# Twelve input-projection tiles per layer computed by the seven-product scheme, in a phase of their own ahead of the mixers (two-layer hybrid trunk, one core)

## The chip, the cores and the metric

The kernel runs on one core of one Trainium2 chip. The metric is device time in microseconds (us). The kernel before takes 1718.01 us (median of 3 runs, 1717.88 to 1718.38). One execution was taken by the hardware profiler; its rows are what the text quotes. PE is the matrix engine (PEld its weight loads), DVE the vector engine, ACT the scalar engine, POOL GpSimd, SP the engine that issues most DMAs. A name such as ACTq is the instruction queue of that engine.

## The reference

Two identical layers work on `x` of 512 tokens by 1024 features in float32:

```python
h = rms_norm(x, ln1[l])
x = x + mixer_block(h, ...)       # u = h @ w_in, four causal mixers, gates, w_up_*, w_out
h = rms_norm(x, ln2[l])
x = x + swiglu(h, w_ffn_in[l], w_ffn_out[l])
...
u = h @ w_in
(fq, fk, fv, ff, gq, gk, gv, glr, gr, rq, rk, rv, rg, z, xbc, dt, gates) = split_cols(u, IN_SPLITS)
...
merged = (g[:, :, 0] * (y_a @ w_up_a) + g[:, :, 1] * (y_b @ w_up_b)
          + g[:, :, 2] * (y_c @ w_up_c) + g[:, :, 3] * (y_d @ w_up_d))
return merged @ w_out
```

The columns of `w_in` feed a forgetting attention (FoX, branch A: fq, fk, fv), a gated linear attention (GLA, B: gq, gk, gv, gr), a retention (C: rq, rk, rv, rg), a Mamba-2 scan (SSD, D: z, and xbc, which passes a four-tap causal convolution per channel), and four sigmoid gates of 1024 columns each. The hidden width of the SwiGLU is 2816.

## The kernel before, in words

Activations lie feature-major: a tile holds 128 features by 512 tokens. PE multiplies a 128x128 block of weights (the stationary side) with such a tile, and a column tile of `w_in` (128 of its columns) takes eight blocks. For precision each product is made three times (`mm3`, L200): every operand is split (`split`, L211) into a high part, a cast to the rounded format fp32r on ACT, and a low part, a subtraction on DVE; PE does high x high, high x low and low x high. One plain column tile is thus 24 matmuls of 512 columns.

Weights stream from HBM in slabs of 8 blocks (512 KB), in the order in which the program asks for them. `load` (L245) puts the DMA on SP's queue into one of two `wr` buffers, `convert` (L257) makes the two parts (ACT, then DVE: lines L212 and L213), `block` (L273) hands a block to PE, and `ahead` keeps two slabs converted in advance.

The input of a layer is normalised late: PE multiplies `x` times the gain (`xh`, `xl`, made by `Norm.feed`, L392, one feature tile at a time), and the row factor 1/rms (`n1.r`: squares, a tree of additions, a matmul with ones, some Newton steps, L366 to L372) is multiplied into each result afterwards. So the first group of four column tiles (`group`, L426) can start while `x` still arrives.

A layer runs as follows.

1. The first group: the four x tiles of xbc (`ps4`, L497). In layer 0 its hook also issues squares and constants. Then `n1.rstd`.
2. Two more xbc tiles, each convolution (`conv`, L475: one tensor-scalar and three multiply-adds on DVE, a Silu on ACT), and the four z tiles, in turns: `proj`, `conv`, `proj`, `conv`. In layer 0 `rotary` (L352) computes the tables of sines. Then the token-major columns (`wide`, L286).
3. The mixers `ssd`, `gla`, `ret`, `fox` are generators with many small steps. `drain` (L462) steps through one, and after each step `pull` (L455) takes fillers from the list `fill` until they are worth `PACE` microseconds: projections (`keep`, `tokmajor`, `silus`), gates (`gate_quad`, L1145: four column tiles and a Sigmoid over all four) and up-projections (`ups`, L1160: a product with `w_up_*`, times the gate, added into `merged`). The fillers give PE work while a mixer's chain is on DVE and ACT.
4. After `fox` the remaining fillers are worked off (L1196): the last four gate tiles of branch A and its eight up-projections, which need FoX's result `ya`. Then `w_out` and the residual.
5. The SwiGLU. Its first four column tiles are plain. The other twenty pairs go in units of four column tiles through the Strassen-Winograd scheme (`strassen`, L1253): a 2x2 arrangement of quarters of the weights and of `x` is multiplied with seven products in place of eight. Each product is 24 `mm3`-matmuls on 256 columns, 168 in a unit. Before that, `sums` (L1226) makes the four combinations t1 to t4 of the input's quarters: eight scales on ACT, eight subtractions of 128x512 on DVE, and four splits. It runs in the hook at k=4 of the plain group. For each unit four quads of 512 KB are loaded (`load(u)`: three `rq` buffers and one `wr` buffer); products 1, 2 and 4 use a quad as it is, with its low part made by ACT (L1286) and an accumulating DMA issued on POOL (L1287); products 6, 5, 7 and 3 use sums made on DVE (L1277) and then split. `collect` copies and adds the results out of PSUM (L1349 on ACT; additions on DVE).

Within each engine a scheduler sets the final order from the program's order and its own estimate of the times; the engines wait for each other by semaphores.

## Time and profile before

| | |
|---|---|
| median of 3 runs | 1718.01 us (1717.88 to 1718.38) |
| time of the profiled execution | 1718.72 us |
| span of the profiled execution | 1717.0 us |
| granted TensorE clock, mean | 0.999 |
| PE busy | 1705.9 us, 99% of the span |
| DVE busy | 1213.2 us, 71% |
| ACT busy | 861.9 us, 50% |
| POOL busy | 225.2 us, 13% |
| moved by DMA | 195.00 MB, mean 114 GB/s |

The span runs from the first to the last event in the trace; 1.7 us of the execution's time lie around it. Busy times overlap between engines. In the rows of a timeline, the columns are start and duration in us, the engine, the line of the kernel, the operation, what it writes and reads by the program's names, and in brackets how long the engine was idle before it and which event ended that. Rows of the chain of waits are start, duration, engine, line and number of instructions. Where consecutive matmuls overlap in the pipeline, their durations exceed their spacing, so a matmul's price is read from the spacing or from a row of the chain that spans many of them. In layer 0 `w_out` lies from 485 to 527 us and the SwiGLU behind it; layer 1 begins at 860.4 us.

### The profile page before, as it was taken

What the parts mean: (1) busy time and instruction counts of PE and PEld (TensorE: products, weight loads), DVE (VectorE), ACT (ScalarE), POOL (GpSimd) and SP (SyncE); (2) the same over time, 40 slices, a digit from 0 to 9 for tenths busy, and PEclk for the clock granted to TensorE, in tenths of its full rate; (3) what the DMA queues carried; (4) which work ended last, traced back from release to release, by engine and by line L of the source; (5) the groups of instructions that cost most, each with busy time, mean ns of one, the idle gap of its engine ahead of it and who ended that gap; (6) DMA issues with size and microseconds to landing.
All of it is one profiled execution on the core that took longest, in us unless ns stands there. A gap on an engine that the chain in (4) does not pass through costs nothing.

```text
span 1717.0 us, 25146 instructions
## 1 busy us (share of the span) xinstructions
PE 1705.9 (99%) x10140; PEld 1484.7 (86%) x10140; DVE 1213.2 (71%) x1683; ACT 861.9 (50%) x1190; POOL 225.2 (13%) x227
## 2 busy tenths in 40 slices
PE   8999999999999999999999999999999999999998
PEld 7878888888888999998988788888888889999998
DVE  5867666768677677675777666767776677767666
ACT  5424543546447646464544254435553574655543
POOL 2032110022101010101010322200221010101010
PEclk9999999999999999999999999999999999999999
DMA  5322222222235657575333222222222365665653
GB/s 199 106 74 74 75 82 78 86 86 74 78 112 143 196 134 186 135 186 121 89 99 115 68 74 75 85 76 89 83 86 82 103 172 161 152 175 139 183 108 102
DMA packets 54693, 195.00 MB, mean 114 GB/s; under 512 B 6064, under 2 KB 6448, under 8 KB 54576
## 3 DMA queue, kind: packets, MB, share of 16 engines
q1 hardware_dynamic: 45072, 160.45, 29.2%
q0 software_dynamic: 8640, 31.46, 10.3%
q8 instruction: 79, 1.29, 0.3%
q10 hardware_dynamic: 864, 1.48, 0.2%
q14 instruction: 38, 0.31, 0.1%
HBM read 191.27 MB, written 2.10 MB: 113 GB/s over the span
## 4 chain that ended last, share of the span: by engine, by line
PE 97%; DVE 1%; DMA 1%; ACT 1%; issue 0%; ACTq 0%; DVEq 0%
PE mm L198 65%; PE mx L198 31%; PE mx L1079 0%; DMA x<-in_x_dram 0%; DMA t<-in_ext_dram 0%; ACT wh L212 0%; DVE wl L213 0%; PE mx L679 0%; DVE t L369 0%; ACT L231 0%; DVE t L836 0%; ACT g L236 0%; DVE t L1168 0%; DVE n L407 0%; PE mx L871 0%
## 5 line engine op out<-in xcount | busy, mean ns | idle before, releaser
L212 ACT CAST wh<-wr 128x1024 fp32r<-128x1024 f32 (+1 forms) x240 | 250.0, 1043 | 378.4 <-PE mm L198 238.0
L198 PE MATMUL mm<-xh,wh 128*128 128x512 f32 (+1 forms) x1184 | 429.2, 362 | 0.9 <-DVE t L1168 0.9
L198 PE MATMUL mm<-xh,wl 128*128 128x512 f32 (+1 forms) x1184 | 428.6, 362 | 0.0
L198 PE MATMUL mm<-xl,wh 128*128 128x512 f32 (+1 forms) x1184 | 427.4, 361 | 0.0
L213 DVE TENSOR_TENSOR wl<-wr,wh 128x1024 fp32r<-128x1024 f32 (+1 forms) x220 | 281.8, 1282 | 119.9 <-ACT wh L212 117.6
L198 PEld LDWEIGHTS mm<-xh,wh 128*128 128x128 f32 x1184 | 222.6, 188 | 35.2 <-DVE t L1168 1.8
L198 PEld LDWEIGHTS mm<-xh,wl 128*128 128x128 f32 x1184 | 222.6, 188 | 35.1 <-issue 1.5
L198 PEld LDWEIGHTS mm<-xl,wh 128*128 128x128 f32 x1184 | 222.6, 188 | 33.7 <-issue 1.1
L198 PE MATMUL mm<-t,wh 128*128 128x512 f32 x448 | 140.3, 392 | 0.0
L198 PE MATMUL mx<-xh,wh 128*128 128x256 f32 (+1 forms) x448 | 136.2, 311 | 3.0 <-ACT wh L212 3.0
L198 PE MATMUL mx<-xl,wh 128*128 128x256 f32 (+1 forms) x448 | 138.5, 309 | 0.0
L1287 POOL DMA_DIRECT2D wl<-in_wsq_dram x60 | 51.9, 864 | 518.0 <-ACT wl L1286 337.1
L198 PE MATMUL mx<-f,wh 128*128 128x512 f32 x352 | 108.3, 390 | 0.0
L198 PE MATMUL mm<-f,wh 128*128 128x512 f32 x352 | 106.0, 390 | 0.0
L198 PEld LDWEIGHTS mm<-t,wh 128*128 128x128 f32 x448 | 83.3, 188 | 17.1
L213 DVE TENSOR_TENSOR l<-rq,wh 128x1024 fp32r<-128x1024 f32 x60 | 73.2, 1219 | 33.1 <-ACT wh L212 18.7
L198 PEld LDWEIGHTS mx<-xh,wh 128*128 128x128 f32 x448 | 84.1, 188 | 9.2 <-ACT wh L212 4.0
L198 PE MATMUL mx<-xh,wl 128*128 128x256 f32 (+1 forms) x288 | 91.0, 327 | 0.0
L198 PEld LDWEIGHTS mx<-xl,wh 128*128 128x128 f32 x448 | 84.2, 188 | 5.1
L198 PE MATMUL mm<-t,wl 128*128 128x512 f32 x224 | 87.5, 390 | 0.0
L212 ACT CAST wh<-rq 128x1024 fp32r<-128x1024 f32 x60 | 62.9, 1049 | 43.9 <-PE mm L198 21.5
L198 PEld LDWEIGHTS mm<-f,wh 128*128 128x128 f32 x352 | 66.1, 188 | 13.5
(275 smaller groups left out, 3457.2 us busy)
## 6 DMA issues: line engine op xcount, KB each, us to landing
wr<-in_wst_dram SPq DMA_DIRECT2D x216, 512.0 KB, 3.5
rq<-in_wsq_dram SPq DMA_DIRECT2D x60, 512.0 KB, 5.3
wl<-in_wsq_dram POOLq DMA_DIRECT2D x60, 512.0 KB, 7.1
wr<-in_wsq_dram SPq DMA_DIRECT2D x20, 512.0 KB, 7.3
out_dram<-x SPq DMA_DIRECT2D x8, 256.0 KB, 2.0
x<-in_x_dram SPq DMA_DIRECT2D x3, 512.0 KB, 7.2
wr<-in_wst_dram SPq DMA_DIRECT2D x4, 256.0 KB, 5.6
x<-in_x_dram SPq DMA_DIRECT2D x2, 256.0 KB, 4.5
```

The costliest lines, as they stand in the source:

```text
L198: T.matmul(o, lhsT=l, rhs=r, start=start, stop=stop, skip_group_check=True)
L212: A.copy(out=hi, in_=src)
L213: V.tensor_tensor(out=lo, in0=src, in1=hi.bitcast(F32), op=ALU.subtract)
L1287: G.dma_start(out=lo, in_=wsq[j], accum_op=ALU.add)
```

## The change

Twelve of a layer's plain `w_in` column tiles go through the seven-product scheme, as three units of four: (x4, x5 | z0, z1), (z2, z3 | gq0, gq1), (gk0, gk1 | gr0, gr1). They run in a phase ahead of the mixers, right behind the first group of four x tiles.

- `strassen`, `sums` and `rights` (the table of right-hand sides, earlier inside `layer`) become functions for either matrix. In the front phase t4 has buffers of its own, since `x` times gain (`xh`, `xl`) is needed afterwards; in the SwiGLU it overwrites a quarter of it, as before.
- The hook of the first group, at k=4, does the squares and constants (layer 0 only) and then `sums(tb1, ...)` and `begin(-2)`: the loads of the first unit's quads and the early low parts.
- The three units follow, then the six convolutions one behind the other, then the token-major columns, and the mixers. In layer 0 `rotary` stands right ahead of `drain(ssd(), ...)`.
- The front phase needs buffers: `front()` opens an outer set (`kp`, eight tiles of 128x2x512) and an inner one (`tq`, `ep`, `rp`, `lp`) that is closed before the mixers. The eight tiles of `kp` hold first the scaled inputs and sums, then the units' results, then, two columns at a time, gates and the merged sum (before: `gp`, tiles of four). The pool of the mixers' tiles falls from 33 to 24.
- Since gq, gk and gr are there already, the fillers shift forward: gates of branch D and rv, rg ahead of `ssd`; one gate quad of branch A (`gate_quad(0, 1)`) goes from behind `fox` to ahead of `drain(fox(), ...)`; `PACE` falls by 7 to 8%.
- 24 quads join the stream of quads (80 to 104), and 12 slabs a layer leave the plain stream.

The core of the diff:

```diff
-PACE = (4.5, 5.0, 5.0, 7.5)
+PACE = (4.2, 4.6, 4.6, 6.9)
...
-FRONT = 26 * 8 + 24 + 2 * 16 + 32 * 8 + 80 + 64 + 2 * PLAIN * KD
+FRONT = 14 * 8 + 24 + 2 * 16 + 32 * 8 + 80 + 64 + 2 * PLAIN * KD
...
-QUADS = DEPTH * (NF - PLAIN) // 2 * 4
+QUADS = DEPTH * (3 + (NF - PLAIN) // 2) * 4
...
-    def mixers():
-        return phase(gp=2, vp=2, bd=1, tp=33)
+    def front():
+        outer = phase(g=64, kp=8)
+        return outer, phase(tq=1, ep=4, rp=5, gl=64, lp=2)
...
+        def front_done(u, a, b):
+            both(a)
+            both(b, 0.125 if u == 1 else None)
+            if u == 0:
+                cin[4:6] = a[:, 0], a[:, 1]
+                act(out=b, in_=b, func=AF.Silu)
+                sz[:2] = b[:, 0], b[:, 1]
...
+        cols = [(C_X + 4 * P, C_Z), (C_Z + 2 * P, C_GQ), (C_GK, C_GR)]
+        begin, run = strassen("w_in", l, [tuple(pairs_of(c) for c in u) for u in cols], tb1, KT, True, front_done)
...
         def first():
-            for k in range(KD):
-                n1.square(k)
-            constants()
-
-        ps4 = group("w_in", l, [C_X + P * i for i in range(4)], n1, KD, first if l == 0 else None)
+            if l == 0:
+                for k in range(KD):
+                    n1.square(k)
+                constants()
+            sums(tb1, PR("ln1"), KT)
+            begin(-2)
+
+        ps4 = group("w_in", l, [C_X + P * i for i in range(4)], n1, KD, first)
         n1.rstd(True)
...
+        run()
+        scope.close()
+        scope = phase(vp=2, bd=1, tp=24)
...
         for i in (4, 5, 0, 1, 2, 3):
-            cin[i] = scaled(ps4[i] if i < 4 else proj("w_in", l, C_X + P * i, n1, KD))
-        conv(4, cin[4])
-        conv(5, cin[5])
-        for i in range(4):
-            sz[i] = scaled(proj("w_in", l, C_Z + P * i, n1, KD))
-            act(out=sz[i], in_=sz[i], func=AF.Silu)
             conv(i, cin[i])
...
-        fill += [keep(gq, j, C_GQ + P * j, 0.125) for j in range(2)] + [keep(gk, j, C_GK + P * j) for j in range(2)]
-        fill += silus([C_GR, C_GR + P, C_RG, C_RG + P])
+        fill += gate_quad(3, 0) + tokmajor(rv, C_RV) + silus([C_RG, C_RG + P])
         fill += [keep(rq, j, C_RQ + P * j) for j in range(2)] + [keep(rk, j, C_RK + P * j) for j in range(2)]
+        if l == 0:
+            rotary()
         drain(ssd(), PACE[0])
...
-        fill += mix(gate_quad(2, 0), up_of(1, 1)) + mix(gate_quad(2, 1), up_of(2, 0)) + mix(gate_quad(0, 0), up_of(2, 1))
+        fill += mix(gate_quad(2, 0), up_of(1, 1)) + mix(gate_quad(2, 1), up_of(2, 0)) + mix(gate_quad(0, 0), up_of(2, 1)) + gate_quad(0, 1)
         drain(fox(), PACE[3])
-        fill += mix(gate_quad(0, 1), up_of(0, 0)) + up_of(0, 1)
+        fill += up_of(0, 0) + up_of(0, 1)
```

How the order on the engines changes is shown at three places. The first is PE at the start of layer 0, behind the first group. Before, the sum for 1/rms (`mm_315`, `mm_322`) is followed by the next plain projection (`mm_342`), whose right-hand sides `xh`, `xl` the first group has used already:

```order
L198 MATMUL mm_315<-n_316,cr 128x512
L198 MATMUL mm_315<-n_317,cr 128x512
L198 MATMUL mm_322<-cs,n_222 128x1 x4
L198 MATMUL mm_342<-xh_134,wh_287 128x512
L198 MATMUL mm_342<-xl_135,wh_287 128x512
L198 MATMUL mm_342<-xh_134,wl_288 128x512
```

Now product 1 of the first unit (banks `mm_423` and `mm_424`, 256 columns, weights `wh_400`) surrounds the end of the group, and product 6 (weights `wh_404`, `l_409`, right-hand side the combination t2) and product 7 (`wh_487`, t3) come next:

```order
L203 MATMUL mm_424<-xh_141,wh_400 128x256
L203 MATMUL mm_424<-xl_142,wh_400 128x256
L203 MATMUL mm_424<-xh_141,wl_307 128x256
L203 MATMUL mm_423<-t2h_173,wh_404 128x256
L203 MATMUL mm_423<-t2l_174,wh_404 128x256
L203 MATMUL mm_423<-t2h_173,l_409 128x256
...
L203 MATMUL mm_423<-t3h_175,wh_487 128x256
L203 MATMUL mm_423<-t3l_176,wh_487 128x256
L203 MATMUL mm_424<-t3h_175,wh_487 128x256
```

So what comes behind the group needs sums of inputs and sums of weights, where before it needed the inputs alone.

The second place is ACT in the same stretch. Before, the last casts of the group's slabs (`wh_194`, `wh_257`) stand among the last scaled inputs (`xh`) and squares (`n_238`, `n_241`):

```order
L236 ACTIVATE xh_134<-x,pr 128x512 x2
L236 ACTIVATE n_238<-x 128x512
L212 CAST wh_194<-wr_114 128x1024
L236 ACTIVATE n_241<-x 128x512
L212 CAST wh_257<-wr_255 128x1024
L212 CAST n_316<-n_222 128x512
L212 CAST wh_287<-wr_285 128x1024
```

Rows now are the casts of the group's slabs (`wh_153`, `wh_207`, `wh_315`), and between them the scaled inputs of `sums` (`k_270` and so on), the casts of t1 to t4, the early low parts (L514) and the high parts of the first products:

```order
L241 ACTIVATE k_270<-x,pr 128x512 x2
L217 CAST wh_153<-wr_115 128x512 x2
...
L217 CAST wh_207<-wr_120 128x1024
L217 CAST t1h_171<-k_279 128x1024
...
L514 ACTIVATE wl_307<-rq_299 128x1024
L514 ACTIVATE wl_310<-rq_301 128x1024
L217 CAST t2h_173<-k_284 128x1024
L217 CAST t3h_175<-k_289 128x1024
L217 CAST t4h_177<-k_294 128x1024
L217 CAST wh_315<-wr_313 128x1024
```

The cast of the group's last slab (`wh_315`) now stands behind all of these.

The third place is PE at the end of `fox` in layer 0. Before, behind the last product with the values (into `mx_3931`) come gate tiles (`mm_4139`, `mm_4185`), and only then the halves of the up-projections that need FoX's last heads (`t_4082`):

```order
L198 MATMUL mx_3931<-t_4071,t_2606 128x128
L198 MATMUL mx_3931<-t_4072,t_2606 128x128
L198 MATMUL mm_4139<-xh_134,wh_4090 128x512
L198 MATMUL mm_4139<-xl_135,wh_4090 128x512
L198 MATMUL mm_4139<-xh_134,wl_4091 128x512
...
L198 MATMUL mm_4185<-xl_135,wh_4160 128x512
L198 MATMUL mm_4119<-t_4082,wh_4090 128x512
L198 MATMUL mm_4171<-t_4082,wh_4122 128x512
```

Now the same halves (`t_4588`) stand directly behind it:

```order
L203 MATMUL mx_4423<-t_4577,t_2911 128x128
L203 MATMUL mx_4423<-t_4578,t_2911 128x128
L203 MATMUL mm_4625<-t_4588,wh_4595 128x512
L203 MATMUL mm_4645<-t_4588,wh_4595 128x512
L203 MATMUL mm_4659<-t_4588,wh_4595 128x512
```

The other halves of those four tiles, which need the first heads only, have moved ahead of the last product with the values.

## The prediction

> **What bounds the kernel now.** I read the busy times and the chain of waits on the profile's page first, then the chain in order of time, then PE's waits.

> ```profile
> PE 1705.9 (99%) x10140; PEld 1484.7 (86%) x10140; DVE 1213.2 (71%) x1683; ACT 861.9 (50%) x1190; POOL 225.2 (13%) x227
> PE 97%; DVE 1%; DMA 1%; ACT 1%; issue 0%; ACTq 0%; DVEq 0%
> ```

> PE is busy for all but 11 us, and it is 97% of the chain that ended last. So whatever shortens PE's work shortens the kernel, as long as PE keeps being fed; and whatever PE has to wait for is added in full, since there is no idle time that could swallow it. Two rows of the chain in order of time give PE's prices:

> ```profile
> 740.58 8.16 PE mm L198 x72
> 860.39 21.77 PE mx L198 x96
> ```

> 72 matmuls of 256 columns (three products of the SwiGLU) take 8.16 us, 0.1133 us each; 96 of 512 columns take 21.77 us, 0.2267 us each. A matmul costs its columns, and half as many cost half.

> How full are the engines that feed PE? This is busy time by stretch (PE, PEld, DVE, ACT, POOL):

> ```profile
> 12.84:25.18 12.34, 10.94 (x47) 8.36 (x46) 12.15 (x13) 7.97 (x13) 6.19 (x5) 1.00 0.50 177
> 860.39:875.72 15.33, 15.33 (x69) 12.69 (x69) 15.33 (x19) 8.87 (x12) 5.14 (x3) 1.00 0.35 103
> 527.00:549.00 22.00, 22.00 (x105) 18.34 (x104) 19.66 (x22) 19.07 (x25) 3.18 (x3) 1.00 0.64 186
> 84.00:160.00 76.00, 76.00 (x433) 59.52 (x432) 51.39 (x81) 28.83 (x44) 24.47 (x19) 1.00 0.23 70
> 560.00:650.00 90.00, 90.00 (x652) 84.34 (x651) 63.56 (x76) 49.89 (x68) 7.11 (x9) 1.00 0.64 163
> ```

> The steady SwiGLU (560 to 650) runs the seven-product scheme with PE full and DVE at 71%. But at both layer starts DVE is full already: 12.15 of 12.34 us, and 15.33 of 15.33. At the start of the SwiGLU (527 to 549) the same `sums` fit, with DVE and ACT at 89% and 87%. That difference decides this case.

> **The change part by part.**

> *PE's work.* A unit of four plain column tiles is 4 x 24 = 96 matmuls of 512 columns, 21.76 us; by the scheme 7 x 24 = 168 of 256 columns, 19.04 us. Saved: 2.72 us a unit, and six units (three a layer) give **-16.3 us**. Nothing else is removed from PE.

> [...] In the page's costly groups a weight load looks longer than a 256-column matmul's spacing:

> ```profile
> L198 PEld LDWEIGHTS mm<-xh,wh 128*128 128x128 f32 x1184 | 222.6, 188 | 35.2 <-DVE t L1168 1.8
> ```

> The scheme has 168 loads in place of 96. If loads lay between matmuls, a unit would be 168 x (113 + 188) = 50.6 us against 96 x (227 + 188) = 39.8, 10.7 us more; six units, +64 us. The trace rules it out: 72 matmuls in 8.16 us leave 113 ns for each pair, less than one load. [...]

> *The start of layer 0.* `sums` and the first unit's preparation now lie beside the first group. Their prices stand in the SwiGLU's start, by timeline and by groups:

> ```profile
> 535.20 1.28 DVE L1240 TENSOR_TENSOR f<-f,f 128x512 f32<-128x512 f32 x2
> 537.61 1.21 DVE L213 TENSOR_TENSOR t1l<-f,t1h 128x1024 fp32r<-128x1024 f32 x1
> 538.75 1.21 DVE L213 TENSOR_TENSOR t2l<-f,t2h 128x1024 fp32r<-128x1024 f32 x1
> L1277 DVE TENSOR_TENSOR rq<-rq,rq 128x1024 f32<-128x1024 f32 x2 | 2.4, 1222 | 0.0
> L236 ACT ACTIVATE f<-x,pr 128x512 f32<-128x512 f32 x8 | 5.1, 710 | 0.0
> L1286 ACT ACTIVATE wl<-rq 128x1024 fp32r<-128x1024 f32 x3 | 3.2, 1054 | 0.0
> L212 ACT CAST t1h<-f 128x1024 fp32r<-128x1024 f32 x1 | 1.0, 1036 | 0.0
> L1349 ACT COPY e<-mm 128x256 f32<-128x256 f32 x1 | 0.4, 372 | 0.0
> ```

> DVE gets eight subtractions at 0.60 us from start to start (the pair at 535.20) = 4.8, four low parts at 1.14 (537.61 to 538.75) = 4.6, and ahead of product 6 three weight sums at 1.22 = 3.7: 13.1 us. ACT gets 5.1 + 4 x 1.04 + 3.2 = 12.5. When does PE want product 6? PE's rows at the end of the group:

> ```profile
> 31.58 0.64 PE L198 MATMUL mm<-n,cr 128*128 128x512 f32 x2
> 32.06 0.95 PE L198 MATMUL mm<-cs,n 128*128 128x1 f32 x8
> 32.87 0.48 PE L198 MATMUL mm<-xh,wh 128*128 128x512 f32 x1
> ```

> Product 1 (24 x 0.1133 = 2.72) would begin at 32.87 at the latest, so product 6 is wanted at 35.6. DVE's rows from 12.84 on, where it begins to run full:

> ```profile
> 12.84 0.69 DVE L407 TENSOR_TENSOR n<-n,n 128x512 f32<-128x512 f32 x1
> ...
> 25.92 0.69 DVE L213 TENSOR_TENSOR n<-n,n 128x512 fp32r<-128x512 f32 x1 [0.74 <-ACT n L212]
> ```

> Its own work from there is 12.15 + 0.69 = 12.8, plus 13.1: 12.84 + 25.9 = 38.8, and then ACT casts the sum, 1.04: 39.8. That is with DVE never waiting: at least 4.2 us late. It will wait: DVE and ACT feed each other in turn (cast, low part, sum), the casts of the group's slabs now stand behind scales and early low parts on ACT, the last one behind all of them, and its DMA behind six others on SP, so the group itself ends later. I add 3.3 us for that, estimated from the 2.7 us by which the third slab's cast moves behind four scales at 0.62 to 0.71. Product 7 reads a cast that stands on ACT behind a copy of product 6's bank: half of product 6 (1.36), copy (0.37), cast 1.04 and low part 1.22 are 4.0 against product 6's 2.72, and DVE owes the Newton steps by then: +3. Layer 0's start: **+10.5 us** (4 to 13).

> *The start of layer 1.* DVE is still adding the residual of the layer before:

> ```profile
> 870.25 0.68 DVE L1424 TENSOR_TENSOR x<-x,f 128x512 f32<-128x512 f32 x1
> ...
> 874.51 1.21 DVE L213 TENSOR_TENSOR wl<-wr,wh 128x1024 fp32r<-128x1024 f32 x1
> 876.91 0.69 DVE L409 TENSOR_TENSOR n<-n,n 128x512 f32<-128x512 f32 x1 [1.19 <-POOL n L407]
> 878.34 0.69 DVE L213 TENSOR_TENSOR n<-n,n 128x512 fp32r<-128x512 f32 x1 [0.74 <-ACT n L212]
> ```

> The last `x` tile, which half of the combinations need, is there 10.5 us after the group begins. DVE full until 875.7, less the low part at 874.51 (it belongs to the next projection, 1.2), plus two of 0.69, plus 13.1, is 889.0, with the cast 890.0. PE wants product 6 at 860.39 + 21.77 + 0.6 for the sum of squares (two matmuls of 512 columns, 0.45, and small ones) + 2.72 = 885.5. So 4.5 us late at least; waits in turn and product 7 as above, with fewer casts in between, +3.5: **+8 us** (4 to 10). Were it as at the SwiGLU's start, this and the term before would be about 0.

> ```profile
> 527.06 16.50 PE mx L198 x72
> ```

> ```profile
> 552.20 0.39 PE L198 MATMUL mm<-t2h,wh 128*128 128x256 f32 x1
> ```

> The first row, of the chain, is that group's beginning; there product 6 starts 25.1 us after it, on time. Its cover is that DVE had the residual behind it.

> *The end of FoX.* The gate tiles that stood behind the last value product are gone from there. In layer 0 now:

> ```profile
> 459.20 0.46 PE L198 MATMUL mx<-t,t 128*128 128x256 f32 x3
> 459.70 0.58 ACT L1094 COPY t<-mx 64x512 f32<-64x512 f32 x1 [3.43 <-PE mx L198]
> 460.31 0.68 DVE L1095 TENSOR_TENSOR t<-mx,t 64x512 f32<-64x512 f32 x1 [2.79 <-ACT t L1094]
> 461.03 0.62 ACT L212 CAST t<-t 128x512 fp32r<-128x512 f32 x1 [0.75 <-DVE t L1095]
> 461.68 0.69 DVE L213 TENSOR_TENSOR t<-t,t 128x512 fp32r<-128x512 f32 x1 [0.69 <-ACT t L212]
> ```

> From the last value product (ends 459.66) to the last heads' high part is 2.0 us, to the low part 2.7; gate matmuls cover it. In the new order the up-projections that need it come next, so PE waits 2.0, works 0.9 on four high parts, and has the low one on time; the last value products too come with less between them and their exponentials. I take 2.6 a layer, **+5.2 us** (2 to 10).

> *Convolutions and `ssd`.* Before, six convolutions lay between projections; now they come in a row:

> ```profile
> L480 DVE SCALAR_TENSOR_TENSOR t<-t,pr,t 128x511 f32<-128x511 f32 (+2 forms) x18 | 12.8, 743 | 0.0
> L477 DVE TENSOR_SCALAR t<-t,pr 128x512 f32<-128x512 f32 x6 | 3.1, 537 | 0.0
> L724 DVE TENSOR_TENSOR t<-cr,dts 128x512 fp32r<-128x512 f32 x8 | 9.5, 1204 | 0.1
> L737 DVE TENSOR_TENSOR t<-t,t 128x512 f32<-128x512 f32 x8 | 6.6, 823 | 5.3 <-ACT t L236 5.3
> ```

> That is 15.9 us of DVE in one go (in layer 0 with the rotary tables), and `ssd`'s decays (16.1 us) queue behind it, while about as many fillers cover it as before. If fillers cover it, 0; if half of the convolutions end up bare, 8. `ssd` has DVE at 51.39 of 76 us, nearer to the covered case: **+4 us** for both layers, 3 of it in layer 0.

> The mixers' other fillers move within full PE time and the six units' loads are 24 quads like those of the steady SwiGLU: 0, covered by DVE's 29% of slack there.

> *Sum.* -16.3 + 10.5 + 8 + 5.2 + 4 = +11.4 us. On the profiled execution's 1718.7 that is 1730.1; the median lies 0.7 lower, so **1730 us** rounded.

> **The rivals.**

> 1. *The starts are covered (faster).* If the scheduler's order lets DVE reach product 6's sums when product 1 ends, as at the SwiGLU's start, terms two and three fall away: -16.3 + 5.2 + 3 = -8, **1710 us** (1706 to 1714). For it: the row at 552.20, the same code. Against it: DVE full at both starts. It decides at product 6's first matmul, 35.6 us and 885.5 us. 0.20.
> 2. *Nothing is left.* Every wait comes out at its lower bound: 4.2 + 4.5 for the starts, 4 for FoX, 2 for `ssd`: -1.6, **1717 us** (1715 to 1721). It asks that DVE never waits for ACT, which did wait in the rows above. 0.13.
> 3. *The mixers become DVE's (slower still).* Fewer fillers and all convolutions in a block: `ssd` at its upper bound of 8 in place of 4, and 3 more in each of `gla`, `ret` and `fox` over both layers, beside the main terms: +24.4, **1742 us** (1736 to 1748). For it: 32.6 us of projections leave the mixers in each layer. Against: `ssd` at 68% DVE. 0.13.
> 4. *Weight loads in the way*, 1718 + 64 = **1782 us**: 0.01, by the row at 740.58.

> **How the numbers follow.** The forecast, 1722 to 1738 us by its bounds, has 0.53. A measurement of this kernel can tell about 0.2% (3.4 us) from no change. Rival 1 and a sixth of rival 2 are faster: 0.22. The rest of rival 2 is the same: 0.11. The forecast, rivals 3 and 4 are slower: 0.67. The range from 1709 to 1741 us leaves out the lower part of rival 1 and the upper part of rival 3, together under 0.2.

> **What would show it.** In the new profile: PE idle ahead of product 6 and product 7 at about 38 to 50 us and 25 us into layer 1, released by casts on ACT or low parts on DVE, with DVE over 90% busy in the 30 us before; a gap of 2 to 3 us behind the last value product in each layer; units of 19.0 us without gaps from product 2 on. PE's idle time in all would grow from 11 us to some 38, and its busy time fall by 16. If PE shows no gap ahead of product 6, rival 1 is right. If the gaps lie in `ssd`, rival 3 is. If a unit takes more than 19.04 us with PE busy throughout, the first term is wrong.

## The result, and the profile after

The changed kernel takes 1782.15 us (median of 4 runs, 1780.70 to 1785.21) against 1718.20 us: 1.0374 times the time before, with a 95% interval of 1.0356 to 1.0392. It is slower, as forecast, but by 64 us where 12 were predicted, and above the range's end of 1741. The profiled execution took 1782.34 us with a span of 1780.6 us, 63.6 more than before.

The page's busy times of the changed kernel, and the engines' shares of the chain that ended last:

```profile
PE 1722.7 (97%) x10572; PEld 1505.2 (85%) x10572; DVE 1264.6 (71%) x1755; ACT 967.0 (54%) x1338; POOL 254.7 (14%) x245
PE 90%; DVE 4%; ACT 4%; issue 1%; DMA 1%; POOL 0%; DVEq 0%; POOLq 0%; ACTq 0%
```

PE's idle time grew from 11.1 to 57.9 us. PE's busy time should have fallen by 16.3 us and rose by 16.8. The other columns explain that. These are stretches of the changed kernel (PE, PEld, DVE, ACT, POOL, granted clock, DMA share, GB/s), first the starts, mixers and ends of FoX, where PE isn't full:

```profile
0.00:60.00 60.00, 44.05 (x214) 36.50 (x215) 39.18 (x51) 41.85 (x59) 11.43 (x15) 0.94 0.67 209
340.00:392.00 52.00, 47.52 (x238) 36.81 (x237) 38.25 (x61) 26.24 (x38) 4.66 (x3) 0.93 0.21 61
495.00:520.00 25.00, 21.41 (x89) 17.10 (x88) 14.56 (x23) 11.59 (x17) 0.29 (x1) 0.86 0.21 65
895.00:950.00 55.00, 45.18 (x261) 39.10 (x260) 45.28 (x60) 39.04 (x54) 15.57 (x8) 0.97 0.56 148
1240.00:1272.00 32.00, 27.00 (x100) 19.57 (x99) 28.20 (x41) 19.60 (x28) 4.67 (x3) 0.89 0.18 52
1375.00:1395.00 20.00, 16.41 (x70) 13.15 (x69) 9.92 (x17) 10.08 (x15) 0.29 (x1) 0.83 0.18 53
```

Then `ssd` and `gla` of both layers apart, and the front units:

```profile
180.00:215.00 35.00, 33.11 (x207) 24.21 (x206) 22.75 (x33) 14.72 (x21) 11.20 (x9) 0.95 0.17 50
215.00:232.00 17.00, 12.73 (x47) 10.07 (x46) 13.97 (x21) 9.70 (x17) 0.52 (x1) 0.80 0.16 60
1060.00:1098.00 38.00, 38.00 (x236) 28.82 (x235) 27.64 (x36) 16.54 (x23) 11.63 (x8) 1.00 0.21 69
1098.00:1112.00 14.00, 10.30 (x41) 8.24 (x41) 12.18 (x19) 8.10 (x13) 0.00 (x0) 0.88 0.14 39
64.00:91.00 27.00, 27.00 (x240) 27.00 (x240) 19.76 (x23) 19.92 (x27) 3.93 (x5) 1.00 0.76 148
```

Two stretches of the kernel before, over the same times as the first two rows above (before, the passage from `ret` to FoX lies some 50 us earlier, and from 290 to 360 us PE is idle for 0.45 us):

```profile
0.00:60.00 60.00, 55.63 (x248) 45.91 (x249) 41.64 (x57) 29.24 (x42) 9.94 (x14) 1.00 0.48 166
340.00:392.00 52.00, 51.47 (x243) 42.67 (x242) 38.51 (x66) 26.24 (x41) 12.67 (x14) 1.00 0.30 92
```

A stretch loses its length less PE's busy time, and also its length times the clock that is missing: a matmul at half clock counts as busy but takes nearly twice its time (from 223.53 to 228.22 us, at a granted clock of 0.50, the matmuls stand 0.43 us apart; behind 228.63, at 1.00, 0.23). So the rows give, over what before lost in the same work:

| stretch | idle, us | clock, us | sum | predicted |
|---|---|---|---|---|
| start of layer 0 (0 to 60) | 16.0 - 4.4 = 11.6 | 60 x 0.06 = 3.6 | 15.2 | 10.5 |
| start of layer 1 (895 to 950) | 9.8 | 55 x 0.03 = 1.7 | 11.5 | 8 |
| ends of FoX (495, 1375) | 3.6 + 3.6 | 3.5 + 3.4 | 14.1 | 5.2 |
| convolutions and `ssd` (180, 1060) | 1.9 + 0 | 1.7 + 0 | 3.6 | 4 |
| `gla` (215, 1098) | 4.3 + 3.7 | 3.4 + 1.7 | 13.1 | 0 |
| from `ret` to FoX (340, 1240) | 4.5 - 0.5 + 5.0 | 3.6 + 3.5 | 16.1 | 0 |
| PE's work | | | -16.3 | -16.3 |
| sum | | | 57.3 | 11.4 |

That is 57 of the 63.6 us; the other 6 lie in many places and aren't assigned here. Over the whole kernel the mean clock fell from 0.999 to 0.985, 25 us more of missing clock. That way of counting is an upper bound, since a slow clock costs nothing while PE is idle: between the first matmul and the last the clock stood at half for 51.2 us, and PE was busy in 46.5 of them, which cost 23 us. The clock column adds up to 26, so the table accounts for some 54 us, and 9 stay open.

PE's waits in the changed kernel (in all, times, longest, us):

```profile
PE mm L203 <- ACT t L217: 12.1, 4, 4.3
PE mx L203 <- ACT t L217: 7.6, 4, 2.6
PE mx L203 <- DVE wl L218: 7.0, 2, 4.5
PE mx L203 <- ACT wh L217: 6.9, 3, 3.8
```

The weights' parts (`wh`, `wl`) are the starts. Most of the mixers' waits are for `t`, a tile of a mixer's chain that is cast on ACT before PE can use it. PE's timeline at the longest of them, in `gla` of layer 0:

```profile
222.94 0.79 PE L203 MATMUL mm<-t,wh 128*128 128x512 f32 x1 [4.27 <-ACT t L217]
223.53 0.63 PE L203 MATMUL mm<-xh,wh 128*128 128x512 f32 x1
...
228.22 0.56 PE L203 MATMUL mm<-xh,wl 128*128 128x512 f32 x1
228.63 0.39 PE L203 MATMUL mm<-xh,wh 128*128 128x512 f32 x1
228.86 0.40 PE L203 MATMUL mm<-xl,wh 128*128 128x512 f32 x1
```

The up-projection of branch D needs `ssd`'s output. Before, rv and gates stood ahead of it, now it stands among the first fillers of `gla`. PE is idle for 4.27 us, and after that its matmuls stand 0.43 us apart, for gates that wait for nothing, until 228.63, where they are back at 0.23. The wait thus costs 4.3 us and then 2.7 (13 matmuls in 5.69 us, which at 0.227 us each take 2.95). What ACT casts there comes late from DVE, which multiplies `ssd`'s output by its row factor (L1002) and is busy for 13.97 of the 17.00 us from 215 to 232:

```profile
222.27 1.28 ACT L217 CAST t<-t 128x512 fp32r<-128x512 f32 x2 [2.13 <-DVE t L1002]
```

Where `ret` ends, ACT's timeline and PE's:

```profile
370.62 1.04 ACT L217 CAST wh<-wr 128x1024 fp32r<-128x1024 f32 x1 [4.95 <-PE mm L203]
371.57 0.61 ACT L217 CAST t<-t 128x512 fp32r<-128x512 f32 x1
372.09 0.63 ACT L241 ACTIVATE t<-t 128x512 f32<-128x512 f32 x1
372.75 0.62 ACT L217 CAST t<-t 128x512 fp32r<-128x512 f32 x1
```

```profile
373.42 0.51 PE L203 MATMUL mx<-t,cr 128*128 128x512 f32 x1 [2.60 <-ACT t L217]
374.18 0.93 PE L203 MATMUL mx<-t,cr 128*128 128x512 f32 x2 [0.26 <-DVE t L218]
375.33 3.16 PE L203 MATMUL mx<-t,cr 128*128 128x512 f32 x5 [0.22 <-DVE t L218]
```

ACT stands for 4.95 us behind a weight cast that waits for PE to finish with its buffer. Then the squares of FoX's queries and keys and their casts come one after the other, and PE waits for each. In the kernel before, ACT did such squares from 309 to 321 us, between weight casts, while PE was busy.

At the end of FoX, ACT's and PE's timelines:

```profile
499.21 1.28 ACT L236 ACT_TABLE_LOAD   x1
500.50 1.06 ACT L241 ACTIVATE k<-k 128x1024 f32<-128x1024 f32 x1
...
502.41 1.05 ACT L241 ACTIVATE k<-k 128x1024 f32<-128x1024 f32 x1
503.48 1.28 ACT L236 ACT_TABLE_LOAD   x1
504.77 0.97 ACT L217 CAST t<-mx 128x512 fp32r<-128x512 f32 x2
```

```profile
505.41 0.39 PE L203 MATMUL mx<-t,t 128*128 128x256 f32 x1 [1.21 <-ACT t L217]
...
509.21 2.50 PE L203 MATMUL mm<-t,wh 128*128 128x512 f32 x5 [2.04 <-ACT t L217]
```

Two Sigmoids with a table load on either side stand ahead of the last casts; the wait at 509.21 is the one that was forecast.

### The profile page after: what moved, and what is told of

Same layout as the page of the kernel before. It is cut to its first block, busy times and chain, and to the rows that moved or that the text cites. A ratio compares the mean times of both kernels' runs of the same rounds, so it can differ in the third digit from the quotient of the medians.

```text
span 1780.6 us, 26301 instructions
## 1 busy us (share of the span) xinstructions
PE 1722.7 (97%) x10572; PEld 1505.2 (85%) x10572; DVE 1264.6 (71%) x1755; ACT 967.0 (54%) x1338; POOL 254.7 (14%) x245
## 3 DMA queue, kind: packets, MB, share of 16 engines
q8 instruction: 83, 1.36, 0.3%
## 4 chain that ended last, share of the span: by engine, by line
PE 90%; DVE 4%; ACT 4%; issue 1%; DMA 1%; POOL 0%; DVEq 0%; POOLq 0%; ACTq 0%
PE mm L203 58%; PE mx L203 31%; DVE wl L218 1%; ACT wh L217 1%; ACT t L217 1%; ACT t L241 1%; ACT k L241 0%; ACT L236 0%; DVE xl L399 0%; POOL n L411 0%; DMA wr<-in_wst_dram 0%; PE mx L1281 0%; DVE x L1466 0%; DVE f L1465 0%; ACT n L241 0%
## 5 line engine op out<-in xcount | busy, mean ns | idle before, releaser
L203 PE MATMUL mm<-xh,wh 128*128 128x512 f32 (+1 forms) x1040 | 370.6, 356 | 1.0 <-DVE k L1356 1.0
L203 PE MATMUL mm<-xh,wl 128*128 128x512 f32 (+1 forms) x1040 | 369.3, 355 | 0.0
L203 PE MATMUL mm<-xl,wh 128*128 128x512 f32 (+1 forms) x1040 | 368.5, 354 | 0.0
L218 DVE TENSOR_TENSOR wl<-wr,wh 128x1024 fp32r<-128x1024 f32 (+1 forms) x196 | 245.9, 1255 | 112.3 <-ACT wh L217 110.0
L203 PEld LDWEIGHTS mm<-xh,wh 128*128 128x128 f32 x1040 | 197.8, 190 | 28.8 <-DVE k L1356 1.2
L203 PEld LDWEIGHTS mm<-xh,wl 128*128 128x128 f32 x1040 | 197.1, 190 | 27.7 <-issue 0.5
L203 PEld LDWEIGHTS mm<-xl,wh 128*128 128x128 f32 x1040 | 197.3, 190 | 27.2 <-issue 1.1
L203 PE MATMUL mx<-xh,wh 128*128 128x256 f32 (+1 forms) x544 | 164.1, 307 | 7.4 <-ACT wh L217 6.9
L203 PE MATMUL mx<-xl,wh 128*128 128x256 f32 (+1 forms) x544 | 166.1, 305 | 0.0
L203 PE MATMUL mm<-t,wh 128*128 128x512 f32 x448 | 146.4, 405 | 15.9 <-ACT t L217 12.1
L218 DVE TENSOR_TENSOR l<-rq,wh 128x1024 fp32r<-128x1024 f32 x78 | 95.2, 1221 | 47.6 <-ACT wh L217 33.4
L217 ACT CAST wh<-rq 128x1024 fp32r<-128x1024 f32 x78 | 81.8, 1049 | 54.4 <-PE mm L203 23.8
```

Of the source, the lines that this page charges most:

```text
L203: T.matmul(o, lhsT=l, rhs=r, start=start, stop=stop, skip_group_check=True)
L217: A.copy(out=hi, in_=src)
L218: V.tensor_tensor(out=lo, in0=src, in1=hi.bitcast(F32), op=ALU.subtract)
```

## The experiments

The first theory: each of these waits stands where the change took cover away (sums at the starts, a gate quad from FoX's end, fillers ahead of D's up-projections), and giving the cover back takes the wait away. The second: ACT is late, for it loads its tables 71 times in place of 41, 1.28 us each. The third, formed later: the mixers are short of matrix work as a whole, as 12 of a layer's tiles are done ahead of them. Against all three stands a rival: the mixers' own chains on ACT and DVE, and the tiles in which they pass, set the waits whatever PE is given to do. In each experiment's timing the kernel before ran on the same chip, at about 1718 us; ratios are against it.

### The starts

Without sums: the four combinations of the input are replaced by quarters of the input, so the eight scales, eight subtractions and four splits are left out.

```diff
-        tb1 = rights(n1, True)
+        tb1 = rights(n1, False)
+        tb1.update(t1=tb1["b21"], t2=tb1["b22"], t3=tb1["b11"])
...
-            sums(tb1, PR("ln1"), KT)
```

> The changed kernel without the sums of the input in the front phase: t1 to t4 are replaced by quarters of the input itself, so eight scales, eight subtractions and four splits are left out in each layer. Theory 1 (the starts wait because DVE and ACT are full): idle at the two starts falls by most of its 17 and 13 us over before; 18 less (12 to 24), 1764. Rival (the starts wait for the quads' loads and the sums of weights): at most 5 less, 1777 or more.

Measured: 1761.34 us, 1.0252 (1.0237 to 1.0267), 20.8 less than the changed kernel. Its start of layer 1, by stretch:

```profile
895.00:935.00 40.00, 38.78 (x270) 35.71 (x269) 30.09 (x41) 28.25 (x39) 7.94 (x8) 1.00 0.77 206
```

PE lacks 1.2 us there in place of 9.8, at full clock. In layer 1 the sums cause the start's waits, as the prediction said. In layer 0 they do so in part: the wait in `gla` that stood at 218.67 comes 9.2 us earlier, but from 0 to 45 us alone PE is still idle for 8.9 us (16.0 from 0 to 60 us with the sums, 4.4 before the change), at a clock of 0.89. The longest wait there, 5.1 us, is for the cast of the group's last slab, which in this version stands on ACT behind the work on 1/rms.

Two units per layer in place of three, with gk and gr as plain tiles between the first group and the units (product 6 comes 22 us later for the sums; PE has 5.4 us more to do):

```diff
-        cols = [(C_X + 4 * P, C_Z), (C_Z + 2 * P, C_GQ), (C_GK, C_GR)]
+        cols = [(C_X + 4 * P, C_Z), (C_Z + 2 * P, C_GQ)]
...
+        t = pair(C_GK)
+        gk[:] = t[:, 0], t[:, 1]
+        begin(-2)
+        t = pair(C_GR)
```

> The changed kernel with two units in the front phase; gk and gr go back to plain column tiles, four of them, placed between the first group and the units, so that PE has 21.8 us of work there that needs neither sums of inputs nor sums of weights. PE's work rises by 2 x 2.72 = 5.4 us. Theory 1 (the starts wait because PE has nothing plain to do while DVE and ACT make the sums): the waits at the starts (23 and 13 us with the slow matmuls behind them, 6 and 0 of that in the kernel before) fall to some 8 in all; 22 less and 5.4 more, 1766 (1758 to 1772). Rival (the starts wait for something in the units themselves, such as the quads' loads or a bank): no wait less, 1787.

Measured: 1769.74 us, 1.0303 (1.0288 to 1.0319): 12.4 less although PE does more. By the spacing of PE's matmuls (waits and half-clock matmuls together, with what before lost there as well) the starts fell from 23 and 13 us to 13 and 6.

### The ends of FoX

The gate quad back behind FoX, as before:

```diff
-... + mix(gate_quad(0, 0), up_of(2, 1)) + gate_quad(0, 1)
+... + mix(gate_quad(0, 0), up_of(2, 1))
         drain(fox(), PACE[3])
-        fill += up_of(0, 0) + up_of(0, 1)
+        fill += mix(gate_quad(0, 1), up_of(0, 0)) + up_of(0, 1)
```

> The changed kernel with the last gate quad of branch A put back behind FoX, in turns with the first half of its up-projections, as before the change. Theory 1 (the added time is PE waiting at places where the new order of fillers leaves a mixer's end uncovered, and after each such wait PE runs at half clock for some microseconds): the 4.8 and 5.1 us of idle and the 2.7 and 1.6 us of slow matmuls at the end of FoX go, 1782 falls by 13 (10 to 15) to about 1769. Rival (only the bare chain behind the last value product is exposed, 2.6 us a layer, as predicted): 5 less, 1777. Rival 2 (the wait moves to another place): no change.

Measured: 1783.64 us, 1.038 (1.0364 to 1.0395): no change. By the spacing of PE's matmuls, FoX's end loses 4.0 us in place of 6.7 in layer 1, and 8.4 in place of 7.4 in layer 0. Moving the quad in the list of fillers doesn't give the cover back, so the first theory fails here.

The two Sigmoids of a gate quad together, behind its fourth column tile, so that tables are loaded 55 times in place of 71:

```diff
-                    if i % 2:
-                        act(out=st["t"], in_=st["t"], func=AF.Sigmoid)
+                    if i == 3:
+                        for t in gates[b][-2:]:
+                            act(out=t, in_=t, func=AF.Sigmoid)
```

> The changed kernel with the Sigmoids of a gate quad issued together, both tiles behind the fourth projection, so that ACT changes its table half as often for them: 55 table loads in the program in place of 71 (41 before the change), 16 x 1.28 = 20.5 us less of ACT. Theory 2 (the change halved the gate tiles to two columns and so doubled the table loads, and these stand between FoX's exponentials and the casts that PE waits for): the waits at FoX's ends and around ret shrink by 1 to 2 us each, 6 less in all (3 to 12), 1776. Rival (ACT is 54% busy and takes the loads in its idle time): within 3 of 1782.

Measured: 1782.56 us, 1.0388 (1.0368 to 1.0407): no change. The groups of table loads, of the changed kernel and then of this one:

```profile
L236 ACT ACT_TABLE_LOAD x62 | 79.5, 1283 | 1.1
```

```profile
L236 ACT ACT_TABLE_LOAD x46 | 59.0, 1283 | 0.8
```

Nine more loads, in both, stand on another line. 20.5 us less work for ACT bought nothing. The second theory falls.

### The wait in `gla`

fq and the gate quad first, and D's up-projections last in `gla`:

```diff
-        fill += mix(gate_quad(3, 1), up_of(3, 0)) + [keep(fq, j, C_FQ + P * j) for j in range(2)]
+        fill += [keep(fq, j, C_FQ + P * j) for j in range(2)] + gate_quad(3, 1) + up_of(3, 0)
```

> The changed kernel with the fillers of gla in another order: the two fq projections and the gate quad first, and the up-projections of branch D, which need the output of ssd, last. Theory 1: the waits of 4.4 and 3.9 us at the first up-projection and the slow matmuls behind them (2.2 and 1.0) go: 11 less (8 to 13), 1771. Rival (DVE is the bound in ssd and gla, so the wait only moves): within 3 of 1782.

Measured: 1777.22 us, 1.0352 (1.0335 to 1.0369): 5 less. Both waits in `gla` are all but gone, 13 us by the table; 2.5 us of new idle time in each layer stand at the start of `ret`, where fq has been spent, and the mean clock is 0.986 (0.985 in the changed kernel). Cover was moved, not made.

Eighteen matmuls whose results are overwritten, put into the wait in `gla` in each layer (8.2 us of work for PE in all):

```diff
+                    if b == 3 and d == 0:
+                        for _ in range(18):
+                            mm(ps, n1.hi[:, 0, :P], n1.hi[:, 0], True, True)
```

> The changed kernel with 18 matmuls of 512 columns on data that is there already, written into the bank of the first up-projection of branch D and overwritten by it: 4.1 us of work that adds nothing to the result, placed where PE waits 4.4 and 3.9 us in gla. Theory 1's second half (idle time itself lowers the clock afterwards): the granted clock behind the place is 1.0, the matmuls there are 0.227 apart in place of 0.427, and the time falls by 1 to 3 us, 1779 to 1781. Rival (the slow matmuls have another cause, or the wait is not at this place but in the work): spacing there stays 0.427 and the time stays or rises by up to 8.

Measured: 1776.11 us, 1.034 (1.0324 to 1.0355): 6 less, with 8.2 us more to do. The stretch that answers to 215 to 232 above:

```profile
215.00:232.00 17.00, 17.00 (x78) 14.13 (x78) 14.15 (x22) 8.67 (x15) 0.52 (x1) 1.00 0.12 37
```

Full, and at a clock of 1.00 in place of 0.80. So the idle time was what lowered the clock here: the useless work filled 8.0 us in which PE had stood idle, and took the slow matmuls behind the wait away, which is the gain. In the changed kernel the 4.27 us of this wait were followed by a spacing of 0.43 us up to 228.63, 5.7 us later; 2.60 us of idle time, ahead of the matmul at 373.42, were followed by half clock too, from 375.36 to 382.18.

### Several at once

The three edits to the mixers together (a quad's Sigmoids together, the quad behind FoX, fq first in `gla`); the same with two units; and this with gates and up-projections exchanged in their alternation and the sums issued behind the first group:

> The changed kernel with the Sigmoids in pairs, the last gate quad of branch A behind FoX as before, and the two fq projections ahead of the gates and up-projections in gla. Theory 1 with theory 2 (thin cover and table loads in the mixers): the waits in gla go (12 us with the slow matmuls, less 3 that move), FoX's ends fall by half (7): 16 less, 1766 (1760 to 1772). Rival (the waits move on to the next place, since DVE's chains bound the mixers): 6 less or fewer, 1776 or more.

> The two-unit kernel with all three edits of the mixers. If starts and mixers are separate causes, their gains add: 1782 - 16 - 16 = 1750 (1742 to 1760). If the waits only move, less than 20 below 1782.

> The two-unit kernel with the edits of the mixers and the exchange of gate and up-projection, and with the sums of the input issued behind the first group, not in its middle, since four plain column tiles now lie between group and units. Theory 1: the slabs of the first group are no longer late (13 us of waits at layer 0's start fall to 6, those of the kernel before; 7 us at layer 1's to 1), and the change from ret to FoX is covered (15 less): 1769 - 13 - 15 = 1741 (1735 to 1752). Rival (the waits move on): 1760 or more.

Measured: 1777.46 us, 1.0344 (1.0324 to 1.0365); 1768.93, 1.0291 (1.0275 to 1.0306); 1770.74, 1.0306 (1.029 to 1.0321). None is clearly better than the best of its parts (1777.22 and 1769.74). In the last one the start of layer 0 is down to 12 us by the spacing of PE's matmuls, but 2.4 us of idle time a layer appear at the start of `ret`, and the idle time from `ret` to FoX, which was to be covered, is 8.5 and 8.7 us (4.5 and 5.0 in the changed kernel). The gains don't add: the first theory names the places rightly, but not what is scarce.

The exchange alone, for the wait from `ret` to FoX:

```diff
-        fill += mix(gate_quad(1, 0), up_of(3, 1)) + mix(gate_quad(1, 1), up_of(1, 0))
+        fill += mix(up_of(3, 1), gate_quad(1, 0)) + mix(up_of(1, 0), gate_quad(1, 1))
```

> The changed kernel with up-projection and gate exchanged in the alternation of two pairs of fillers that run from ret into FoX, so that at FoX's first step a gate tile of 5.4 us is taken, as before the change, and not an up-projection of 2.7 us. Theory 1 (at the change from ret to FoX the filler that happens to stand there is too short for the chain of squares and casts): the waits of 9.7 us a layer there fall to 2, 15 less, 1767 (1763 to 1773). Rival (ACT's queue is blocked there by a weight cast that waits for PE, whatever the filler): within 4 of 1782.

Measured: 1783.1 us, 1.0373 (1.0355 to 1.039): no change. And 45 overwritten matmuls a layer, ahead of the matmuls on FoX's squares, of D's up-projections and of FoX's (20.4 us of PE work in both layers):

```diff
+                for _ in range(18 if q is fsq[0] else 0):
+                    mm(ps, n1.hi[:, 0, :P], n1.hi[:, 0], True, True)
...
+                    for _ in range({(3, 0): 18, (0, 0): 9}.get((b, d), 0)):
```

> The kernel with the 18 added matmuls in gla, with 18 more at the change from ret to FoX (in the bank of the first sum of squares) and 9 at the end of FoX (in the bank of the first up-projection of branch A), all overwritten. That is 20.4 us of work that adds nothing. If idle time itself lowers the clock afterwards, the slow matmuls at these places (1.6 + 0.4 and 2.7 + 1.6 us besides gla's) go too: 4 less than with gla's alone, 1772. Rival (no such cause, or the chains only start later): 1776 or more.

Measured: 1779.17 us, 1.0355 (1.034 to 1.0371), 3 less with 20 more to do. The waits at FoX's ends and in `gla` shrink; from `ret` to FoX PE is idle for 5.3 and 6.1 us, in more pieces, against 4.5 and 5.0 without the added matmuls.

### How much matrix work the mixers have, and how fast it is handed out

The amounts per step as before the change:

```diff
-PACE = (4.2, 4.6, 4.6, 6.9)
+PACE = (4.5, 5.0, 5.0, 7.5)
```

> The changed kernel with the four rates at which fillers are taken (PACE) as before the change, 7 to 8% higher. Rival (the mixers wait because fillers come too slowly): the waits at the end of ret (10 us a layer) and in gla (6 us) shrink by half, 14 less, 1768. Theory 1 (they wait because of which filler stands at the place, and the total of fillers is the same): within 4 of 1782, with waits at other places.

Measured: 1806.51 us, 1.0512 (1.0493 to 1.0531), 24 more. With fewer fillers they run out ahead of the mixers' ends: 6.1 and 7.3 us idle at FoX's ends (3.6 each in the changed kernel), and a single wait of 7.1 us from `ret` to FoX in each layer. So the 7 to 8% by which the change lowered the amounts were needed.

Five plain column tiles a layer whose results nobody uses (54.4 us of PE work in both layers), with the amounts of before and the gate quad behind FoX:

```diff
+        fill += gate_quad(3, 0) + tokmajor(rv, C_RV) + [(TILE, dummy)] + silus([C_RG, C_RG + P])
...
+        fill += [(TILE, dummy)] * 2 + mix(gate_quad(3, 1), up_of(3, 0)) + ...
...
+        fill += ... + mix(gate_quad(1, 1), up_of(1, 0)) + [(TILE, dummy)] * 2
```

> The changed kernel with five dummy column tiles (24 matmuls of 512 columns on data that is there, results unused) among the fillers of each layer: one in ssd, two at the head of gla's, two at the end of ret's; the last gate quad of branch A behind FoX, and the rates as before the change. PE gets 10 x 5.44 = 54 us of added work. Theory 3: the mixers are as long as their own chains, and the added work fills waits; the time rises by 15 at most, 1785 to 1797. Rival (the waits have other causes): all of it is added, with the 25 us that the higher rates alone cost: 1836 or more.

Measured: 1868.53 us, 1.0876 (1.0859 to 1.0892): 86 more, 32 beyond the added work. Its largest wait of PE:

```profile
PE mm L203 <- DVE t L1372: 11.7, 2, 5.9
```

The amounts alone had cost 24 us; with matrix work enough for them the waits should have gone, and this one grew from 2.2 us to 11.7. The third theory, as it stands, is refuted.

One unit per layer: x4, x5, z0 and z1 by the scheme, z2 and z3 as plain tiles between group and unit, the sums behind the group, gq, gk and gr as fillers again, with amounts of 5.2, 5.5, 5.5 and 7.5, a quad's Sigmoids together and the last gate quad behind FoX; then the same with 4.6, 5.8, 5.8 and 7.2:

```diff
-        cols = [(C_X + 4 * P, C_Z), (C_Z + 2 * P, C_GQ), (C_GK, C_GR)]
+        cols = [(C_X + 4 * P, C_Z)]
...
+        z2 = proj("w_in", l, C_Z + 2 * P, n1, KD)
+        sums(tb1, PR("ln1"), KT)
+        begin(-2)
+        z3 = proj("w_in", l, C_Z + 3 * P, n1, KD)
...
+        fill += kpair(C_GQ, is_q, 0.125) + kpair(C_GK, is_k) + kpair(C_GR, is_r)
```

> One unit in the front phase (x4, x5, z0, z1), z2 and z3 as plain column tiles between the first group and the unit, gq, gk and gr back among the fillers (now at the head of ssd's), the last gate quad of branch A behind FoX, Sigmoids in pairs, rates 5.2, 5.5, 5.5, 7.5. The mixers have all of their earlier matrix work again, with the small pools and two-column gates of the change. PE's work is 2 x 2.72 = 5.4 us under that of the kernel before. Theory 3 (the mixers' chains need the matrix work of gq, gk and gr as cover): the 50 us of waits in the mixers fall to 15 or less; 1718 - 5 + 15 + 3 for the starts = 1731 (1715 to 1742). Rival (the pools and gates of the change slow the mixers): the waits stay, 1765 or more.

> The one-unit kernel with the fillers spread otherwise: rates 4.6, 5.8, 5.8, 7.2, so that ssd takes fewer and gla and ret more. Theory 3: within 8 of the other distribution, with waits moved between ssd and ret. Rival: 1765 or more.

Measured: 1757.48 us, 1.0231 (1.0214 to 1.0248), and 1770.82, 1.0308 (1.0293 to 1.0323). The first lies between the two forecasts, the second beyond the 8 us that the theory allowed. With one unit the waits of `ssd` and `gla` are gone:

```profile
175.00:240.00 65.00, 65.00 (x409) 54.67 (x408) 44.49 (x76) 31.45 (x48) 10.90 (x13) 1.00 0.26 82
350.00:380.00 30.00, 25.76 (x91) 18.34 (x90) 26.70 (x39) 19.29 (x28) 4.66 (x3) 0.89 0.15 48
480.00:500.00 20.00, 15.71 (x67) 12.30 (x66) 11.29 (x19) 8.59 (x14) 0.29 (x1) 0.83 0.11 29
```

Those from `ret` to FoX (350) and at FoX's end (480) are as large as with three units. And 13 us hang on the amounts per step alone, the only difference between the two.

### The mixers' tiles

The pool of the mixers' tiles fell from 33 to 24 with the change. Two fewer:

```diff
-        scope = phase(vp=2, bd=1, tp=24)
+        scope = phase(vp=2, bd=1, tp=22)
```

> The changed kernel with 22 tiles in the mixers' pool in place of 24. Theory 4 (the pool is too small, so that FoX's squares and the last heads' work cannot start before ret's tiles are free): waits at ret to FoX and elsewhere in the mixers grow, 8 more (5 to 20), 1790. Rival (24 are enough, the order is set by other waits): within 4 of 1782.

Measured: 1825.99 us, 1.0621 (1.0605 to 1.0637), 44 more. PE's largest waits there:

```profile
PE mx L203 <- ACT t L217: 27.8, 8, 10.5
PE mm L203 <- ACT t L217: 15.3, 4, 5.8
```

These are the first two rows of the changed kernel's list, which had 7.6 and 12.1. One tile more, for which the positions are loaded late, into a tile of the pool:

```diff
+        posi = TT(I32)
+        nc.scalar.dma_start(out=posi, in_=pos)
...
-        scope = phase(vp=2, bd=1, tp=24)
+        scope = phase(vp=2, bd=1, tp=25)
```

> The changed kernel with 25 tiles in the mixers' pool; the space comes from the positions, which are loaded into a tile of the pool when rotary needs them and not kept. Theory 4: the waits at ret to FoX shrink, 4 less (2 to 8), 1778. Rival: within 3 of 1782.

> The one-unit kernel with 25 tiles in the pool, as above. Theory 4: 4 less than its 1757.5, 1753. Rival: within 3 of 1757.5.

Measured: 1783.61 us, 1.0379 (1.036 to 1.0398), no change, with three units; and 1743.02, 1.0145 (1.0128 to 1.0162) with one, 14.5 less than the one-unit kernel of 24 tiles. The second one also has the amounts of before and rv, the gates of D and fq in another order, so the 14.5 us aren't the tile's alone. Its end of FoX and its largest wait:

```profile
480.00:500.00 20.00, 20.00 (x91) 16.61 (x90) 12.38 (x16) 9.50 (x12) 0.00 (x0) 1.00 0.26 81
```

```profile
PE mx L203 <- ACT t L1254: 7.0, 2, 3.5
```

FoX's ends are full, and from `ret` to FoX PE is still idle for 6.1 and 6.3 us, now mostly for another cast of FoX's preparation. This is the best of the versions with units ahead of the mixers, and 25 us slower than the kernel without them. None of the versions here is as fast as that one.

## Why the prediction was right or wrong

**PE's work, -16.3: right.** In the row of 64 to 91 us, 240 matmuls of 256 columns, with 240 weight loads that overlap them, take 27.00 us, 0.1125 each. So rival 4 is wrong, though the time that it gave, 1782, is the measured one: weight loads aren't in the way. That PE's busy time rose by 16.8 us nevertheless is for the most part half-clock work (23 of the 33 us between forecast and measurement), which that forecast did not have.

**The starts, +10.5 and +8: right in mechanism, somewhat small.** 21.4 us of waiting against 18.5, and 5.3 of missing clock. Leaving the sums out took 20.8 back, though in layer 0 a wait for a slab's cast stayed. The layer-0 start also shows the DMA that the prediction put behind six others. It is issued only at 28.12 us, right behind DVE's low part that frees its buffer (25.80 to 28.08), and takes 6.65 us to land; so DVE has a part in it too. ACT's row at the end of the first group:

```profile
34.79 1.04 ACT L217 CAST wh<-wr 128x1024 fp32r<-128x1024 f32 x1 [4.60 <-DMA wr<-in_wst_dram]
```

In layer 1 the wait stands earlier than forecast, in the group itself. PE's and DVE's rows there:

```profile
920.60 1.37 PE L203 MATMUL mx<-xh,wl 128*128 128x512 f32 x4 [4.46 <-DVE wl L218]
```

```profile
915.75 1.21 DVE L218 TENSOR_TENSOR t1l<-k,t1h 128x1024 fp32r<-128x1024 f32 x1
916.88 0.68 DVE L472 TENSOR_TENSOR k<-k,k 128x512 f32<-128x512 f32 x1
918.71 0.69 DVE L413 TENSOR_TENSOR n<-n,n 128x512 f32<-128x512 f32 x1 [1.16 <-POOL n L411]
919.32 1.22 DVE L218 TENSOR_TENSOR wl<-wr,wh 128x1024 fp32r<-128x1024 f32 x1
```

The low part of the group's last slab (919.32) stands behind the sums on DVE. For layer 1 the prediction had charged the sums to what follows the group; they also delay the group itself, as it had said for layer 0.

**The ends of FoX, +5.2: right in place, too small.** 7.2 us of waiting, inside the bounds of 2 to 10, and 6.9 of missing clock, which brings it to 14.1. The forecast wait of about 2 us stands at 509.21.

**Convolutions and `ssd`, +4: right.** 3.6, all of it in layer 0, though half of that is missing clock, which the forecast did not have.

**"The mixers' other fillers move within full PE time ... 0, covered by DVE's 29% of slack": the step that failed.** It measured 29 us (`gla` 13.1, from `ret` to FoX 16.1; 17 of them idle time, the rest missing clock). For the fillers the reason given was PE's full time. The slack was an average over the SwiGLU, and both said nothing of a mixer's end, where one chain through ACT and DVE must end before PE can go on. There it matters what stands ahead of the first instruction that needs the mixer's output. The prediction asked that for FoX's end and not for the ends of `ssd` and `ret`, whose fillers were shifted by the same edit. Nor did it price the pool's fall from 33 to 24 tiles. That this pool is close to an edge is shown (two tiles fewer cost 44 us); that its fall from 33 caused the waits is not, for one tile more gave nothing in the changed kernel, and a pool of the old size was not run with it.

**A term that was missing: the clock behind a wait.** Some 23 us over the kernel, in no term and no bound. It is why even the terms with a right wait came out too small. It does not explain the miss alone: without it the time would still be some 1759 us, above the range, mostly because of the step that failed. The bounds of the single terms add up to 1712 to 1743 us, not to the forecast's 1722 to 1738, and don't reach the measured time either. (Rival 2 took 4 us for FoX and 2 for `ssd` as lower bounds; stated were 2 and 0.)

**Rival 3 had the place, and its mechanism in `gla` at most.** The mixers do lose PE's time. In `gla` ACT's cast of `ssd`'s output waits for DVE, which is busy nearly throughout, so DVE has a part in that wait. From `ret` to FoX it isn't the bound: it is busy for 38.25 of 52 us, about as before, and PE waits for ACT. The time is beyond the rival's 1742, since it sized the waits at 3 us for each mixer over both layers.

**What stays open.** Why the passage from `ret` to FoX loses some 6 us or more a layer in every version. The trace shows ACT behind a weight cast that waits for PE, with FoX's squares behind that cast; other fillers (exchanged order, overwritten matmuls) did not end it. Issuing the squares earlier was not tried.

## What to carry to other kernels

Work that is removed from the bounding engine is worth its time only if it wasn't cover; before moving it, find for each chain on the other engines the first instruction that waits for its end, and count what stands ahead of that before and after. When a nearly gapless engine begins to wait, price each wait of some microseconds with the slow stretch behind it as well (4.3 us and then 2.7 in `gla` of layer 0). Scratch tiles and the rate at which fillers are handed out are part of such a change's price: two tiles were worth 44 us here, and 8% of the rate 24.

## What the runs showed of the hardware

That PE's clock falls behind a short wait in the middle of a busy kernel was not expected, and no term had it. Three stretches of the changed kernel:

```profile
34.02:37.43 3.41, 1.54 (x7) 1.29 (x8) 1.64 (x2) 2.64 (x3) 0.00 (x0) 1.00 0.67 135
218.34:221.75 3.41, 0.33 (x2) 0.01 (x1) 3.23 (x6) 1.76 (x4) 0.52 (x1) 1.00 0.04 10
221.75:228.58 6.83, 5.64 (x13) 4.46 (x14) 6.69 (x11) 2.98 (x6) 0.00 (x0) 0.50 0.19 72
```
